# Three score tiles of 1024 keys, and one PSUM bank each for projection and value sums, in a hybrid attention block

## The chip, the cores and the metric

The kernel runs on one core of one Trainium2 chip. The metric is the device time of the program in microseconds (us). The engines are named as in the profile: PE is TensorE's matrix products, PEld its weight loads, DVE is VectorE, ACT ScalarE, POOL GpSimd, SP SyncE (which here only issues DMAs). PE writes its sums into PSUM, which has eight banks of 512 floats for each of its 128 partitions; DVE and ACT read them from there ("drain" them), after which a bank may be filled anew.

## The reference, cut to what matters

One layer over 2048 positions of width 1024, all in float32:

```python
u = rms_norm(x, norm1_w)
dq, dk, dv, sq, sk, sv = split(u @ w_in)
# four heads: two softmax maps each, chunk-causal mask, relative-position bias
attn = softmax(q0 @ k0 * s + bias) - lam * softmax(q1 @ k1 * s + bias)
y_A = rms_norm(attn @ dv) * (1 - lambda_init)
# eight heads of stick-breaking attention, strictly causal
log_1mb = log_sigmoid(-z)                       # z = q @ k * scale
rem = cumsum(log_1mb, reverse=True) - log_1mb
y_B = rms_norm(exp(log_sigmoid(z) + rem) @ sv)
h = x + concat(y_A, y_B) @ w_out
u2 = rms_norm(h, norm2_w)
out = h + (silu(u2 @ w_gate) * (u2 @ w_up)) @ w_down
```

## The kernel before, in words

Matrix products run on 16-bit operands. A float32 operand is split into a high and a low half, and a product of two such operands is three products (high-high, high-low, low-high) summed in one PSUM bank.

**Groups and blocks.** The 2048 queries are 16 blocks of 128 (`i`). The heads are eight groups (`g`): groups 0 to 3 are one differential head each, groups 4 to 7 a pair of stick-breaking heads each. For each group the normalized, transposed input is projected in 16 tiles of 128 positions: `proj_tile` (L314) lets PE make 24 products of 128x384 into a bank with the tag `pj` (L320), and `proj_out` (L334) drains it: the values first (L327 or L329 for the high half, L330 for the low half), then the queries and keys (L341 or L343 in groups 0 to 3, again L327/L329 and L330 in groups 4 to 7). Which of ACT and DVE makes a high half is chosen by a balance of estimated load. In group 0 the input itself is transposed on the way (`fresh_t`, L607; `transposed`, L591, with L594 on PE).

**Scores.** `score_chunk` (L446) multiplies the queries of a block with up to 512 keys (two products, L448) into a bank with the tag `sc`, of which there are four. A block sees the keys up to its own end, taken in stretches of 1024 keys (`b`), and a stretch in chunks of 512 (`c`). The chunks are what the change is about.

- Differential attention (`probs`, L462): DVE copies each chunk out of PSUM with the running maximum (L483; L487 for the last 256 keys, which get the bias); then an exponential on ACT, the difference of the two maps on DVE, and `split_t` (L398), which makes the two halves (L89, L91 or L93 and L98) and transposes them by a DMA into `aT`.
- Stick-breaking attention (`stage_a`, L540): for each chunk ACT makes two sigmoids (L554 into SBUF, L555 in place in PSUM), DVE runs the product from the right as a scan (L557), then multiplies (L558), chunk by chunk from the right. The chunks hang together by one column (`om[:, hi : hi + 1]`). Then `split_t`.

**Value sums.** `pv` (L453) multiplies `aT` with the values into a bank with the tag `yp`, of which there are two (L458); four query blocks share a bank (two in the last group), at 128 columns each. After the fourth block `finish` (L407) takes the squares of the bank (L416 or L418), scales it into `y` (L429), transposes `y` back into the same bank (L431), and drains that to 16 bits (`mo`, L435 on ACT, L436 on DVE).

**PSUM before.** Two banks `pj` (also used by the small sums that set the weights' scales and by the output projection's `po`, L755), four banks `sc` (also used by `transposed`), two banks `yp` (also used once by `build_bias`). In the feed-forward part the six banks of `sc` and `yp` are a ring with the tag `b`, and every fourth call of `pst` (L816) takes a bank `pj`.

**The order of the work.** The program is written as generators. `advance` (L708) emits projection tiles of later groups between the attention blocks, about eight tiles ahead. Then a scheduler that simulates the engines sets the order of the instructions on each engine from these, with priorities (`PRI`), from its own idea of durations and of when each buffer comes free: so the number of banks changes the order. On the chip each engine runs its list strictly in order and waits for semaphores.

The stages follow each other with some overlap. By the trace of the profile the prologue (projection of group 0) lies in 0 to 105 us, differential attention in 105 to 615 us, the stick-breaking attention of groups 4 to 6 (with the beginning of 7) in 615 to 1215 us, the last group with the output projection (`out_proj`, L744, products L761) in 1215 to 1472 us, and the feed-forward part to the end.

Of the kernel before, what the change touches and what calls it, by code (L numbers as in the profile page):

```python
# [11 lines left out]
F32 = mybir.dt.float32  # L12
# [4 lines left out]
ALU = mybir.AluOpType  # L17
# [42 lines left out]
def block(tc, a, out):  # L60
# [3 lines left out]
    with top:  # L64
# [182 lines left out]
        psj = top.enter_context(tc.tile_pool(name="psj", bufs=2, space=PSUM, side="right"))  # L247
# [3 lines left out]
        with ExitStack() as ph1:  # L251
# [4 lines left out]
            bias = s16p.tile([P, 4, 256], F32, name="bias", bufs=1)  # L256

# [202 lines left out]
            def diff_attn(g, G):  # L460
                @pri("at")
                def probs(i):  # L462
# [8 lines left out]
                    for m in range(2):  # L471
                        nx = 0
                        for b in range(nb):
                            n = min(1024, L - 1024 * b)
                            z = z4()
                            for c in range((n + 511) // 512):
                                lo, hi = 512 * c, min(512 * c + 512, n)
                                sc = ps.tile([P, 512], F32, tag="sc", bufs=4, name=nm("sc"))
                                score_chunk(G, sc, i, 2 * b + c, m, (hi - lo) // P)
                                f = min(max(near - 1024 * b - lo, 0), hi - lo)  # L480
                                note("D", 1.05 * (hi - lo) + 200)
                                if f > 0:
                                    DVE.tensor_scalar(z[:, lo : lo + f], sc[:, :f], kz_d[:], None, op0=ALU.mult, op1=ALU.max, accum_out=mx[:, m, nx : nx + 1])  # L483
                                    nx += 1
                                if f < hi - lo:
                                    b0 = 1024 * b + lo + f - (i - 1) * 128
                                    DVE.tensor_tensor_reduce(z[:, lo + f : hi], sc[:, f : hi - lo], bias[:, g, b0 : b0 + hi - lo - f], kz_d[:], -3.0e38, ALU.add, ALU.max, mx[:, m, nx : nx + 1])  # L487
                                    nx += 1
                            zs[m].append((b, n, z))
# [46 lines left out]
            def sb_attn(g, G):  # L536
                last = {}

                @pri("at")
                def stage_a(i, m, b):  # L540
                    L = (i + 1) * 128
                    n = min(1024, L - 1024 * b)
                    be, om = z4(), z4()
                    if b == i // 8:
                        DVE.memset(om[:, n : n + 1], 8192.0)
                    else:
                        DVE.tensor_copy(om[:, n : n + 1], last[m][:, 0:1])
                    last[m] = om
                    for c in range((n - 1) // 512, -1, -1):
                        lo, hi = 512 * c, min(512 * c + 512, n)  # L550
                        w = hi - lo
                        sc = ps.tile([P, 512], F32, tag="sc", bufs=4, name=nm("sc"))
                        score_chunk(G, sc, i, 2 * b + c, m, w // P, b == i // 8 and hi == n)
                        ACT.activation(om[:, lo:hi], sc[:, :w], AF.Sigmoid, scale=G["nkz"][:])  # L554
                        ACT.activation(sc[:, :w], sc[:, :w], AF.Sigmoid, scale=G["kz"][:])  # L555
                        ov = om[:, lo:hi][:, ::-1]
                        DVE.tensor_tensor_scan(ov, ov, sc[:, :w], om[:, hi : hi + 1], op0=ALU.mult, op1=ALU.bypass)  # L557
                        DVE.tensor_tensor(be[:, lo:hi], sc[:, :w], om[:, lo + 1 : hi + 1], ALU.mult)  # L558
                        note("A", 1.7 * w + 400)
                        note("D", 3.15 * w + 350)  # L560
                    return n, split_t(be[:, :n], n, "A", "P")
# [3 lines left out]
                def stage_b(i, m, b, n, aT):  # L565
                    r, k = fq(g, i)
                    if i // k not in ypd:
                        ypd[i // k] = ps.tile([P, 512], F32, tag="yp", name=nm("yp"))
# [22 lines left out]
            def transposed(xn, o):  # L591
                tr = ps.tile([P, 512], F32, tag="sc", bufs=4, name=nm("xtr"))
                for j in range(4):
                    PE.transpose(tr[:, P * j : P * j + P], xn[:, o + P * j : o + P * j + P], id32[:])  # L594
                return tr
# [29 lines left out]
            def build_bias():  # L625
# [5 lines left out]
                for h in range(4):  # L631
                    pt = ps.tile([P, 512], F32, tag="yp", name=nm("bt"))
# [111 lines left out]
            def out_proj():  # L744
                for t in range(NT):
# [8 lines left out]
                    for h in range(2):  # L754
                        po = psj.tile([P, 512], F32, tag="pj", name=nm("po"))  # L755
# [47 lines left out]
        with ExitStack() as ph2:  # L803
# [424 lines left out]
```

## Time and profile before

| | us |
|---|---|
| runs of the kernel | 2783.66, 2777.36, 2782.47 |
| median | 2782.47 |
| span of the profiled execution | 2785.0 |
| busy in it: PE, DVE, POOL, ACT | 2489.9, 2000.8, 1445.2, 1361.8 |
| of it PE on projection products (L320, 3072 of them) | 572.3 |
| of it DVE on the scan (L557, 320 of them) | 355.5 |

The profile is of one execution, and its span of 2785.0 us is that execution's own time, from the first instruction to the last; all times in the trace count from its start. A row of the timeline has the start of an instruction (or of a run of equal ones), how long it took, the engine and line, what it wrote and read with the shapes, and in brackets how long the engine had stood idle before it and whose result it waited for. A row by form has the busy time in all, the mean in ns of one, and the idle time before them. A row of the windows has the stretch, its length, the busy time and count of instructions of PE, PEld, DVE, ACT and POOL in this order, the granted clock of PE as a share of full speed, the share of time that the DMA engines were busy, and GB/s. A row of waits has who waited for whom: the idle time in all, how often, and the longest.

### The profile page before, as it was taken

What the parts mean: (1) busy time and instruction counts of PE and PEld (TensorE: products, weight loads), DVE (VectorE), ACT (ScalarE), POOL (GpSimd) and SP (SyncE); (2) the same over time, 40 slices, a digit from 0 to 9 for tenths busy, and PEclk for the clock granted to TensorE, in tenths of its full rate; (3) what the DMA queues carried; (4) which work ended last, traced back from release to release, by engine and by line L of the source; (5) the groups of instructions that cost most, each with busy time, mean ns of one, the idle gap of its engine ahead of it and who ended that gap; (6) DMA issues with size and microseconds to landing.
All of it is one profiled execution on the core that took longest, in us unless ns stands there. A gap on an engine that the chain in (4) does not pass through costs nothing. (4 is left out here: it accounts for less than half of the span.)

```text
span 2785.0 us, 45469 instructions
## 1 busy us (share of the span) xinstructions
PE 2489.9 (89%) x17084; PEld 1409.0 (51%) x17084; DVE 2000.8 (72%) x3782; ACT 1361.8 (49%) x2543; POOL 1445.2 (52%) x1008
## 2 busy tenths in 40 slices
PE   6998989888878786888889798989999999999998
PEld 4665556555545453557775343444444444444443
DVE  6888879687989989876756877777786644434445
ACT  4665656466878788765644534443442212111121
POOL 2567767665544555546665656565654332322323
PEclk9999999999999897999999999999999999999999
DMA  6788787789999998997796565655658844635534
GB/s 225 199 167 184 147 188 163 164 174 205 198 205 198 192 182 160 190 198 205 197 309 253 184 235 189 221 187 191 240 170 299 327 155 178 227 125 190 211 129 166
DMA packets 649133, 551.91 MB, mean 198 GB/s; under 512 B 506624, under 2 KB 574208, under 8 KB 638672
## 3 DMA queue, kind: packets, MB, share of 16 engines
q1 hardware_dynamic: 647088, 546.92, 71.2%
q8 instruction: 134, 2.20, 0.3%
q0 software_dynamic: 512, 1.36, 0.2%
q10 hardware_dynamic: 1312, 0.72, 0.1%
q14 instruction: 87, 0.71, 0.1%
HBM read 265.27 MB, written 151.52 MB: 150 GB/s over the span
## 5 line engine op out<-in xcount | busy, mean ns | idle before, releaser
L98 POOL TENSOR_TENSOR s<-z,s 128x1024 f16<-128x1024 f32 (+7 forms) x288 | 474.1, 1654 | 334.8 <-ACT s L89 299.3
L320 PE MATMUL pj<-w,xt 128*128 128x384 f16 x3072 | 572.3, 334 | 32.6 <-DVE st L330 11.6
L320 PEld LDWEIGHTS <-xt 128*128 128x128 f16 x3072 | 299.9, 100 | 241.8 <-issue 36.3
L448 PE MATMUL sc<-kT,qT 128*128 128x512 f16 (+3 forms) x1280 | 346.9, 362 | 74.6 <-DVE z L558 34.4
L1034 PE MATMUL pd<-wd,act 128*128 128x512 f16 x1848 | 406.2, 379 | 3.3 <-DVE hs L1040 2.4
L557 DVE TENSOR_TENSOR_SCAN z<-z,sc 128x512 f32<-128x512 f32 (+3 forms) x320 | 355.5, 1112 | 68.6 <-ACT sc L555 65.1
L458 PE MATMUL yp<-v,aT 128*128 128x64 f16 (+1 forms) x4896 | 281.2, 207 | 80.0 <-DMA aT<-s 79.2
L458 PEld LDWEIGHTS <-aT 128*128 128x128 f16 x4896 | 245.2, 102 | 169.4 <-DMA aT<-s 105.1
L936 PEld LDWEIGHTS <-wg 128*128 128x128 f16 x1848 | 183.9, 100 | 264.3 <-issue 58.8
L98 POOL TENSOR_TENSOR hs<-hs,cu 128x512 f32<-128x512 f32 x132 | 170.5, 1297 | 238.2 <-DVE cu L1040 82.6
L936 PEld LDWEIGHTS <-wu 128*128 128x128 f16 x1848 | 181.0, 98 | 222.1 <-issue 9.0
L1034 PEld LDWEIGHTS <-act 128*128 128x128 f16 x1848 | 180.6, 98 | 222.6 <-issue 4.7
L98 POOL TENSOR_TENSOR act<-cg,act 128x512 f16<-128x512 f32 x117 | 160.8, 1385 | 247.7 <-ACT act L992 141.5
L98 POOL TENSOR_TENSOR fst<-fst 128x512 f32<-128x512 f32 x97 | 179.6, 1852 | 167.6 <-DVE wd L215 78.6
L1040 DVE SCALAR_TENSOR_TENSOR hs<-pd,c,hs 128x512 f32<-128x512 f32 x192 | 142.1, 748 | 160.8 <-PE pd L1034 159.1
L89 ACT CAST s<-z 128x384 f16<-128x384 f32 (+7 forms) x216 | 170.1, 788 | 151.5 <-DMA aT<-s 56.4
L554 ACT ACTIVATE z<-sc,c 128x512 f32<-128x512 f32 (+3 forms) x320 | 202.6, 633 | 10.6 <-PE sc L448 6.5
L558 DVE TENSOR_TENSOR z<-sc,z 128x512 f32<-128x512 f32 (+3 forms) x320 | 193.3, 606 | 8.1
L992 ACT CAST act<-cg 128x512 f16<-128x512 f32 x132 | 80.6, 617 | 234.2 <-DVE cg L998 190.9
L555 ACT ACTIVATE sc<-sc,c 128x512 f32<-128x512 f32 (+3 forms) x320 | 194.8, 609 | 0.0
L761 PE MATMUL po<-wo,mt 128*128 128x256 f16 x1536 | 181.3, 276 | 11.0 <-DVE xf L764 6.3
L936 PE MATMUL pm<-X,wg 128*128 128x512 f16 x792 | 179.1, 379 | 1.2 <-ACT bx L1109 1.2
(233 smaller groups left out, 4028.4 us busy)
## 6 DMA issues: line engine op xcount, KB each, us to landing
xt<-xs SPq DMA_DIRECT2D x112, 512.0 KB, 4.4
hs<-hd SPq DMA_DIRECT2D x96, 512.0 KB, 4.3
hd<-hs SPq DMA_DIRECT2D x80, 512.0 KB, 3.2
split<-wg SPq DMA_DIRECT2D x11, 1792.0 KB, 10.5
split<-wu SPq DMA_DIRECT2D x11, 1792.0 KB, 10.3
split<-wd SPq DMA_DIRECT2D x11, 1792.0 KB, 10.4
wg<-split SPq DMA_DIRECT2D x11, 1792.0 KB, 7.3
wd<-split SPq DMA_DIRECT2D x11, 1792.0 KB, 8.4
```

The costliest lines, as they stand in the source:

```text
L89: ACT.copy(dst, src)
L98: (DVE if e == "D" else POOL).tensor_tensor(dst, a_, b_, op)
L320: PE.matmul(pj[:, :384], lhsT=xv[:, xi, kt, :], rhs=G["w"][:, wi, kt, :], start=n == 0, stop=n == 23)
L448: PE.matmul(sc[:, : 128 * w].rearrange("p (t n) -> p t n", n=P), lhsT=G["q"][i // 4][:, 2 - 2 * o + m, i % 4, :], rhs=G["k"][q][:, m, 0:w, ...
L458: PE.matmul(yp[:, y0 : y0 + wd], lhsT=aT[:, a_, :], rhs=v[:, v_ : v_ + wd], start=start and j == 0 and q == 0, stop=stop and j == nb - 1 a ...
L554: ACT.activation(om[:, lo:hi], sc[:, :w], AF.Sigmoid, scale=G["nkz"][:])
L555: ACT.activation(sc[:, :w], sc[:, :w], AF.Sigmoid, scale=G["kz"][:])
L557: DVE.tensor_tensor_scan(ov, ov, sc[:, :w], om[:, hi : hi + 1], op0=ALU.mult, op1=ALU.bypass)
L558: DVE.tensor_tensor(be[:, lo:hi], sc[:, :w], om[:, lo + 1 : hi + 1], ALU.mult)
L761: PE.matmul(po[:, sl], lhsT=mt[:, kt, P * xi : P * xi + P], rhs=wos[2 * h + n][wi][:, kt, :], start=q == 0, stop=q == 23)
L936: PE.matmul(ps_[:].rearrange("p (t n) -> p t n", n=P), lhsT=wv[:, wo, wi, 128 * kt : 128 * kt + 128], rhs=X[xo][:, :, xi, kt, :], start=st ...
L1034: PE.matmul(po[:], lhsT=act[:, ao, xi, 128 * j : 128 * j + 128], rhs=W["d"][:, wo, wi, :], start=start and u == 0 and q == 0, stop=u == nu ...
```

## The change

The banks are dealt out anew: one bank `pj` instead of two, one bank `yp` instead of two, and three score tiles of 1024 floats (two banks each) in place of four of 512. A score tile now holds a whole stretch of up to 1024 keys. PE's products stay at up to 512 columns each, so their number is the same; what DVE and ACT do to the scores (L483, L487, L554, L555, L557, L558) is issued once for each tile and no longer for each chunk. `transposed` takes a score tile and uses half of it. Of the output projection's two half sums one takes the bank `pj` and the other a score tile for the first twelve blocks; the last four take theirs from `pst`. The feed-forward part has a ring of seven, and every eighth call of `pst` takes the bank `pj`. Behind the first added lines the numbers of the lines are shifted by 1 to 6.

```diff
-        psj = top.enter_context(tc.tile_pool(name="psj", bufs=2, space=PSUM, side="right"))
+        psj = top.enter_context(tc.tile_pool(name="psj", bufs=1, space=PSUM, side="right"))
...
+            def scores():
+                return ps.tile([P, 1024], F32, tag="sc", bufs=3, name=nm("sc"))
...
-                            z = z4()
+                            z, sc = z4(), scores()
                             for c in range((n + 511) // 512):
                                 lo, hi = 512 * c, min(512 * c + 512, n)
-                                sc = ps.tile([P, 512], F32, tag="sc", bufs=4, name=nm("sc"))
-                                score_chunk(G, sc, i, 2 * b + c, m, (hi - lo) // P)
-                                f = min(max(near - 1024 * b - lo, 0), hi - lo)
-                                note("D", 1.05 * (hi - lo) + 200)
-                                if f > 0:
-                                    DVE.tensor_scalar(z[:, lo : lo + f], sc[:, :f], kz_d[:], None, op0=ALU.mult, op1=ALU.max, accum_out=mx[:, m, nx : nx + 1])
...
+                                score_chunk(G, sc[:, lo:hi], i, 2 * b + c, m, (hi - lo) // P)
+                            f = min(max(near - 1024 * b, 0), n)
+                            note("D", 1.05 * n + 200)
+                            if f > 0:
+                                DVE.tensor_scalar(z[:, :f], sc[:, :f], kz_d[:], None, op0=ALU.mult, op1=ALU.max, accum_out=mx[:, m, nx : nx + 1])
...
-                        ypd[0] = ps.tile([P, 512], F32, tag="yp", name=nm("yp"))
+                        ypd[0] = ps.tile([P, 512], F32, tag="yp", bufs=1, name=nm("yp"))
...
+                    sc = scores()
                     for c in range((n - 1) // 512, -1, -1):
                         lo, hi = 512 * c, min(512 * c + 512, n)
-                        w = hi - lo
-                        sc = ps.tile([P, 512], F32, tag="sc", bufs=4, name=nm("sc"))
-                        score_chunk(G, sc, i, 2 * b + c, m, w // P, b == i // 8 and hi == n)
-                        ACT.activation(om[:, lo:hi], sc[:, :w], AF.Sigmoid, scale=G["nkz"][:])
-                        ACT.activation(sc[:, :w], sc[:, :w], AF.Sigmoid, scale=G["kz"][:])
-                        ov = om[:, lo:hi][:, ::-1]
-                        DVE.tensor_tensor_scan(ov, ov, sc[:, :w], om[:, hi : hi + 1], op0=ALU.mult, op1=ALU.bypass)
-                        DVE.tensor_tensor(be[:, lo:hi], sc[:, :w], om[:, lo + 1 : hi + 1], ALU.mult)
...
+                        score_chunk(G, sc[:, lo:hi], i, 2 * b + c, m, (hi - lo) // P, b == i // 8 and hi == n)
+                    ACT.activation(om[:, :n], sc[:, :n], AF.Sigmoid, scale=G["nkz"][:])
+                    ACT.activation(sc[:, :n], sc[:, :n], AF.Sigmoid, scale=G["kz"][:])
+                    ov = om[:, :n][:, ::-1]
+                    DVE.tensor_tensor_scan(ov, ov, sc[:, :n], om[:, n : n + 1], op0=ALU.mult, op1=ALU.bypass)
+                    DVE.tensor_tensor(be[:, :n], sc[:, :n], om[:, 1 : n + 1], ALU.mult)
...
             def transposed(xn, o):
-                tr = ps.tile([P, 512], F32, tag="sc", bufs=4, name=nm("xtr"))
+                tr = scores()
...
-                        po = psj.tile([P, 512], F32, tag="pj", name=nm("po"))
+                        if t < 12 and h:
+                            po = scores()[:, :512]
+                        elif t < 12:
+                            po = psj.tile([P, 512], F32, tag="pj", name=nm("po"))
+                        else:
+                            po = pst("po")
...
-                if pst_n[0] % 4:
-                    return ps2.tile([P, 512], F32, tag="b", bufs=6, name=nm(t))
+                if pst_n[0] % 8:
+                    return ps2.tile([P, 512], F32, tag="b", bufs=7, name=nm(t))
```

Since the scheduler reads the buffers, the order of the instructions changes nearly everywhere in the attention. Three places show how.

The first is on PE, where one projection tile (`pj`) ends and the next begins. In the kernel before, in group 0 at the start of differential attention, the last product of one tile stands directly ahead of the first of the next:

```order
L448 LDWEIGHTS qT_739
L448 MATMUL sc_1470<-kT_740,qT_739 128x256
L320 LDWEIGHTS xt_1141
L320 MATMUL pj_1185<-w_172,xt_1141 128x384
L320 LDWEIGHTS xt_1422
L320 MATMUL pj_1427<-w_817,xt_1422 128x384
```

In the changed kernel, in the prologue, three runs of transposes (which are on score tiles) stand between two tiles:

```order
L323 LDWEIGHTS xt_409
L323 MATMUL pj_478<-w_172,xt_409 128x384
L595 MATMUL sc_590<-id_63,z_581 128x128 x4
L595 MATMUL sc_597<-id_63,z_581 128x128 x4
L595 MATMUL sc_643<-id_63,z_634 128x128 x4
L323 LDWEIGHTS xt_462
L323 MATMUL pj_552<-w_172,xt_462 128x384
```

With one bank the scheduler puts other work between a tile and the next where it has some.

The second place is on PE as well, where the value bank is handed over after the first four blocks of group 0. In the kernel before, the value products of the next four blocks (`yp_1488`, the second bank) stand ahead of the transposes of `y` of the first four (`yp_1280`):

```order
L458 LDWEIGHTS aT_1486
L458 MATMUL yp_1488<-v_284,aT_1486 128x128
L431 MATMUL yp_1280<-id_63,y_1401 128x128 x4
L448 LDWEIGHTS qT_1005
L448 MATMUL sc_1760<-kT_507,qT_1005 128x512
```

In the changed kernel the last score and projection products stand there instead, and the next value product comes 65 rows behind these:

```order
L451 MATMUL sc_1740<-kT_740,qT_1005 128x512
L323 LDWEIGHTS xt_1418
L323 MATMUL pj_1423<-w_817,xt_1418 128x384
L434 MATMUL yp_1280<-id_63,y_1397 128x128 x4
L451 LDWEIGHTS qT_1005
L451 MATMUL sc_1747<-kT_1006,qT_1005 128x256
```

The value products that stood ahead of the transposes have moved behind them, and behind the drain of `yp_1280`.

The third place is on DVE in group 4, query block 12 (the scan is listed there as SCALAR_TENSOR_TENSOR of L557, L558 in the changed kernel). Before, scans and multiplies of 512 and 128 columns, with the drains of a projection tile (`pj_10254`) between them:

```order
L545 MEMSET z_9525 128x1
L557 SCALAR_TENSOR_TENSOR z_9478<-z_9478,sc_9488 128x512
L330 SCALAR_TENSOR_TENSOR v_10014<-pj_10254,v_10014 128x2x64
L558 TENSOR_TENSOR z_9477<-sc_9488,z_9478 128x512
L557 SCALAR_TENSOR_TENSOR z_9525<-z_9525,sc_9527 128x128
L330 SCALAR_TENSOR_TENSOR st_10013<-pj_10254,st_10013 128x4x64
L558 TENSOR_TENSOR z_9524<-sc_9527,z_9525 128x128
L547 COPY z_9591<-z_9478 128x1
L557 SCALAR_TENSOR_TENSOR z_9525<-z_9525,sc_9535 128x512
L558 TENSOR_TENSOR z_9524<-sc_9535,z_9525 128x512
```

In the changed kernel:

```order
L547 MEMSET z_9158 128x1
L558 SCALAR_TENSOR_TENSOR z_9158<-z_9158,sc_9160 128x640
L559 TENSOR_TENSOR z_9157<-sc_9160,z_9158 128x640
L547 MEMSET z_9200 128x1
L558 SCALAR_TENSOR_TENSOR z_9200<-z_9200,sc_9202 128x640
L333 SCALAR_TENSOR_TENSOR v_9127<-pj_9231,v_9127 128x2x64
L559 TENSOR_TENSOR z_9199<-sc_9202,z_9200 128x640
L549 COPY z_9261<-z_9158 128x1
L333 SCALAR_TENSOR_TENSOR st_9126<-pj_9231,st_9126 128x4x64
L558 SCALAR_TENSOR_TENSOR z_9261<-z_9261,sc_9263 128x1024
L559 TENSOR_TENSOR z_9260<-sc_9263,z_9261 128x1024
```

The 512 and 128 of a stretch of 640 keys have become one instruction, and the next stretch is one of 1024; the drains of a projection tile (`pj_9231`) still stand between single scans and multiplies.

More of the change, by code (lines that the diff above doesn't have):

```diff
@@ L567, in stage_b @@
                     if i // k not in ypd:
-                        ypd[i // k] = ps.tile([P, 512], F32, tag="yp", name=nm("yp"))
+                        ypd[i // k] = ps.tile([P, 512], F32, tag="yp", bufs=1, name=nm("yp"))
                     yp = ypd[i // k]
@@ L591, in transposed @@
             def transposed(xn, o):
-                tr = ps.tile([P, 512], F32, tag="sc", bufs=4, name=nm("xtr"))
+                tr = scores()
                 for j in range(4):
                     PE.transpose(tr[:, P * j : P * j + P], xn[:, o + P * j : o + P * j + P], id32[:])
-                return tr
+                return tr[:, :512]
             @pri("fr")
@@ L631, in build_bias @@
                 for h in range(4):
-                    pt = ps.tile([P, 512], F32, tag="yp", name=nm("bt"))
+                    pt = ps.tile([P, 512], F32, tag="yp", bufs=1, name=nm("bt"))
                     PE.matmul(pt[:, :384], lhsT=rbb[:, h, :], rhs=oh[0:32, 0:384], start=True, stop=True)
```

14 lines of the change are left out of this document (7 added, 7 removed).

## Prediction

> **What bounds the kernel now.** I read the windows first, cut at the borders of the stages, then two stretches inside the stick-breaking stage:
>
> ```profile
> 0.00:105.00 105.00, 76.89 (x449) 49.70 (x450) 73.14 (x162) 50.73 (x102) 39.24 (x48) 0.93 0.67 215
> 105.00:615.00 510.00, 463.64 (x3628) 295.79 (x3626) 431.98 (x1302) 305.18 (x795) 353.95 (x253) 0.97 0.80 171
> 615.00:1215.00 600.00, 475.90 (x4891) 299.71 (x4888) 528.96 (x952) 467.68 (x905) 306.34 (x199) 0.93 0.96 194
> 1215.00:1472.00 257.00, 229.84 (x2364) 194.50 (x2365) 172.31 (x279) 138.78 (x221) 153.69 (x101) 0.97 0.84 233
> 1472.00:2785.00 1313.00, 1243.60 (x5759) 569.33 (x5756) 794.45 (x1090) 399.41 (x522) 592.01 (x407) 0.98 0.56 203
> ...
> 932.00:982.00 50.00, 33.16 (x384) 20.79 (x383) 47.34 (x73) 40.90 (x71) 28.16 (x15) 0.83 0.94 172
> 1038.00:1112.00 74.00, 46.37 (x483) 26.84 (x484) 70.57 (x107) 63.23 (x110) 40.94 (x25) 0.77 0.87 160
> ```
>
> The feed-forward part is PE's (1244 of 1313 us), the stage ahead of it too (230 of 257). Differential attention is led by PE (464 of 510, 91%), with DVE at 85%. Stick-breaking attention is led by DVE (529 of 600, 88%), PE stands at 79%. In the last two stretches DVE is at 95%, PE at 66 and 63%: there DVE alone sets the pace, and DVE is known to reach 95% where nothing else holds it up. Then the waits, first of differential attention, then of stick-breaking attention:
>
> ```profile
> PEld L458 <- DMA aT<-s: 36.2, 24, 4.2
> ...
> DVE z L483 <- PE sc L448: 18.7, 20, 3.1
> ```
>
> ```profile
> PEld L458 <- DMA aT<-s: 56.3, 50, 3.8
> ...
> PEld L448 <- DVE z L558: 44.3, 40, 2.1
> ...
> DVE z L557 <- ACT sc L555: 35.9, 42, 3.2
> ```
>
> PE waits for transposed probabilities, and in the second stage 44.3 us for a score bank that DVE still holds; DVE waits for sigmoids there.
>
> **Part 1: fewer DVE instructions.** The forms give a fixed cost:
>
> ```profile
> L557 DVE TENSOR_TENSOR_SCAN z<-z,sc 128x512 f32<-128x512 f32 x224 | 284.9, 1272 | 40.4 <-ACT sc L555 38.0 <-PE pj L320 1.6 <-PE sc L450 0.4
> L558 DVE TENSOR_TENSOR z<-sc,z 128x512 f32<-128x512 f32 x224 | 153.4, 686 | 5.6
> ...
> L557 DVE TENSOR_TENSOR_SCAN z<-z,sc 128x128 f32<-128x128 f32 x32 | 15.2, 473 | 15.7 <-ACT sc L555 15.4
> L558 DVE TENSOR_TENSOR z<-sc,z 128x128 f32<-128x128 f32 x32 | 9.2, 288 | 0.8
> ```
>
> ```profile
> L557 DVE TENSOR_TENSOR_SCAN z<-z,sc 128x512 f32<-128x512 f32 x183 | 232.8, 1272 | 20.6 <-ACT sc L555 18.1 <-PE pj L320 1.6 <-PE sc L450 0.4
> ```
>
> ```profile
> L483 DVE TENSOR_SCALAR_CACHE_REDUCE z<-sc,c 128x512 f32<-128x512 f32 x168 | 122.6, 742 | 14.4 <-PE sc L448 12.7 <-POOL s L93 1.0 <-POOL s L98 0.5
> L483 DVE TENSOR_SCALAR_CACHE_REDUCE z<-sc,c 128x128 f32<-128x128 f32 x32 | 10.9, 341 | 1.4 <-POOL s L98 1.4
> ```
>
> The scan goes from 473 to 1272 ns over 384 columns, 2.08 ns a column, so 207 ns at none; the multiply in the same way 155 ns. Two chunks merged save one of each: 0.362 us. Scans fall from 320 to 192, so there are 128 merges; 183 of the 224 scans of 512 columns lie in 615 to 1215 us, which puts 128 x 183/224 = 105 merges there: 38 us, DVE 529 to 491. L483 has 207 ns at no column; 96 of 256 go: 20 us, but in differential attention, where PE leads, so off the path (price zero; 10 if half of it counted). ACT's two sigmoids also lose 128 issues each; ACT stands at 468 of 600, behind DVE, so this is no term of its own.
>
> The Trainium skill ("Perfetto Trace Analysis", section "Optimizing Scalar/DVE Operations") gives the fixed part as some 60 ns on SBUF and 125 on PSUM and says that grouping helps a saturated engine, while an engine that isn't saturated may do better with smaller pieces; an estimate by its figures is 105 x 0.185 = 19 us in place of 38. Rows here say twice that.
>
> What is the 38 us worth? At the present DVE share of 88% the stage takes 491/0.88 = 557 us, 43 less. It could take more of the gain, if the share rises (rival 1).
>
> **Part 2: one bank for projections.** A tile's 24 products take 4.06 us; until its drains end no product of the next tile can start now. PE runs its list in order, so scores, values and SP's and POOL's later steps behind that product wait with it. From the timelines of PE and ACT, prologue and differential attention:
>
> ```profile
> 63.14 3.58 PE L320 MATMUL pj<-w,xt 128*128 128x384 f16 x21
> 66.55 1.04 PE L594 MATMUL xtr<-id,z 128*128 128x128 f32 x8
> 67.42 4.06 PE L320 MATMUL pj<-w,xt 128*128 128x384 f16 x24
> ```
>
> ```profile
> 97.12 0.28 ACT L327 ACTIVATE v<-pj 128x128 f16<-128x128 f32 x1 [2.73 <-PE pj L320]
> ...
> 99.41 0.38 ACT L341 ACTIVATE raw<-pj 128x256 f32<-128x256 f32 x1 [1.05 <-DVE v L330]
> ```
>
> ```profile
> 401.86 0.28 ACT L327 ACTIVATE v<-pj 128x128 f16<-128x128 f32 x1 [0.92 <-PE pj L320]
> 403.70 0.38 ACT L341 ACTIVATE raw<-pj 128x256 f32<-128x256 f32 x1 [1.57 <-DVE v L330]
> ...
> 404.55 0.33 PE L320 MATMUL pj<-w,xt 128*128 128x384 f16 x1
> ...
> 409.67 0.36 ACT L341 ACTIVATE raw<-pj 128x256 f32<-128x256 f32 x1
> ```
>
> The drain takes, from the last product, 99.79 - 97.12 = 2.7 us in the prologue, and in differential attention 404.08 - 401.86 = 2.2 or 410.03 - 404.88 = 5.1. What covers it is work placed between two tiles. Before, 51 of 127 boundaries had none. In the changed order I counted the products between and priced them by their durations here: on average 1.3 us in the prologue (eight transposes are 67.42 - 66.55 = 0.87), 2.6 in differential attention, 2.9 in the stick-breaking stage.
>
> - Prologue: 13 boundaries x (2.7 - 1.3) = +18. No bank is spare there, and PE leads (the bounds: 0 if another wait covers it, 13 x 2.7 = 35 if no cover is in time).
> - Differential attention: 51 boundaries, each between 0 (drain 2.2, cover 2.6) and 5.1 - 2.6 = 2.5; I take 0.8, nearer to the short drain since a scheduler that knows of the one bank has put the drains early: +41 (0 to 128).
> - Stick-breaking attention: here a drain takes longer,
>
> ```profile
> 840.31 0.81 PE L320 MATMUL pj<-w,xt 128*128 128x384 f16 x4
> ...
> 849.61 0.41 DVE L330 SCALAR_TENSOR_TENSOR st<-pj,st 128x256 f16<-128x256 f32 x1
> ...
> 982.60 3.41 PE L320 MATMUL pj<-w,xt 128*128 128x384 f16 x20 [1.27 <-DVE st L330]
> ```
>
> 850.02 - 841.12 = 8.9 us, since DVE puts scans first; even with two banks PE waited for one at 982.60. But what waits is PE, and DVE leads. DVE has enough in hand: a merged tile is 2 x 1272 - 207 + 2 x 686 - 155 = 3.55 us of it, two tiles wait in the ring of three while one is filled: 7.1 us, against 4.06 of projection products and what is left of the drain. And the new order puts the drains between single scans, where the old one had long runs of scans without one (the two 95% stretches above). So 0 here (up to +288, rival 2).
>
> **Part 3: one bank for value sums.** From the last value product to the end of the last drain of the bank:
>
> ```profile
> 459.29 0.55 PE L458 MATMUL yp<-v,aT 128*128 128x128 f16 x7
> ...
> 470.53 0.67 DVE L429 TENSOR_TENSOR y<-yp,yrs 128x512 f32<-128x512 f32 x1
> ...
> 475.92 0.74 DVE L436 SCALAR_TENSOR_TENSOR mo<-yp,c,mo 128x512 f16<-128x512 f32 x1
> ```
>
> 476.66 - 459.84 = 16.8 us. Before, 29 of 35 next value products began inside that time in the other bank; now none can. Up to 471.20 the transposes wait as they did. New is the rest, 5.5 us at most, once in four blocks; the new order has 0.2 to 18 us of PE work there. Differential attention has 16 such places: between 0 and 16 x 5.3 = 85, I take 0.6 each, +10. In the other stage DVE's lead covers it as above. From both terms of differential attention (51) I take off 11: of the 36.2 us that PE waits for `aT` there, a third is time in which `aT` would land during the new waits. So +40 (0 to 190).
>
> **Part 4: the rest.** The score ring's three tiles hold 3072 columns for 2048: part of the 44.3 us of waits for a score bank goes, but DVE leads there, so nothing beyond part 1. SP's and POOL's steps are the same ones in the same number. In the stage from 1215 on the output projection's two half sums have a bank each as before,
>
> ```profile
> L761 PE MATMUL po<-wo,mt 128*128 128x256 f16 x1536 | 181.3, 276 | 11.0 <-DVE xf L764 6.3
> ```
>
> and PE waits 6.3 us for their drain now; +2 for the score tiles being shared with the last group (0 to 10). In the feed-forward part each call of `pst` reuses the bank of eight calls before, with 6 + 2 as with 7 + 1: 0.
>
> **The sum.** +18 + 40 - 43 + 2 + 0 = +17: a span of 2785 + 17 = 2802 us. The median of the runs shown is 2782.5, 2.5 below that span; so **2799 us**. Its own bounds: the prologue's 0 to 35 and the other terms of its size give 2788 to 2835. About 0.2% (5.6 us) is what a measurement of this kernel can tell from no change.
>
> **Rivals.**
>
> 1. *Faster: DVE alone sets the stick-breaking stage.* The evenly mixed order and the deeper ring let DVE run at the 95% of the two stretches: 491/0.95 = 517, -83; with prologue and differential attention at half their price, +30, this is 2785 - 83 + 30 = 2732 of span; with both at full price 2762; with the 2.5 off, some 2750 us between. For it: those stretches. Against it: DVE waits 35.9 us for sigmoids, and these now cover 1024 keys before a scan can begin. Chance 0.37 (with what lies between it and no change).
> 2. *Much slower: one projection bank stops PE in the stick-breaking stage.* If a drain stays at 8.9 us with 2.9 covered, each of the 48 boundaries stops PE for 6 us, and scores and values queue behind it: 288, so PE needs 476 + 288 = 764 us for a stage of 600. With half of the boundaries so it is 476 + 144 = 620, +20, and with prologue, differential stage and the 2 beside it 2785 + 20 + 60 = 2865; with all 3009. I put it at 2880. It decides from the point where PE's stops exceed 557 - 476 = 81 us, 1.7 a boundary. For it: PE's granted clock in the 66 and 63% stretches is 0.83 and 0.77, so that a PE that often stops is also a slower one. Against: the order that mixes drains with scans. The Trainium skill ("Perfetto Trace Analysis", section "Matmuls") says that independent groups of products should rotate through PSUM banks, so that the drain of one overlaps the products of the next, which is this case. Chance 0.11.
> 3. *No change within 0.2%*, the prologue's and the differential stage's price and the saving cancelling: 2777 to 2788. Chance 0.10.
>
> **How the numbers follow.** The forecast has 0.42, rival 1 0.37, rival 2 0.11, rival 3 0.10. Faster is 0.37, same 0.10, slower 0.42 + 0.11 = 0.53. The range takes in the forecast's own (2788 to 2835), rival 3, the greater part of rival 1 down to 2740, and goes up to 2865 for dearer drains; it leaves out the deepest gains and most of rival 2.
>
> **What would show it.** In the profile after: the prologue some 18 us longer, with waits of PE (L323) for the drains L333 and L344 that aren't there now; the differential stage some 40 longer by the same waits; DVE's busy time in the stick-breaking stage down by 38, its share still near 88%, the stage shorter by some 40; the feed-forward part as long as before. The forecast is wrong if the prologue and the differential stage keep their lengths (drains hidden), or if DVE's share rises to 95% (rival 1), or if the stick-breaking stage gets longer with PE waiting for L333 (rival 2).

## The result, and the profile after

The changed kernel takes 3005.7 us (median; 3002.2 to 3009.7), the kernel before 2783.1 in the same comparison: 1.0809 times as long, 95% interval 1.0793 to 1.0825, or 223 us more. The forecast was 2799, the range 2740 to 2865.

For the comparison both executions are cut anew at the same events: the first score product of groups 0, 4 and 7, and the last product of the output projection. Windows of before, then of after:

```profile
0.00:106.00 106.00, 77.89 (x456) 50.30 (x457) 74.10 (x162) 50.73 (x103) 39.24 (x48) 0.94 0.68 216
106.00:614.00 508.00, 462.13 (x3612) 294.67 (x3610) 430.01 (x1295) 304.17 (x793) 353.95 (x253) 0.97 0.80 171
614.00:1134.00 520.00, 412.39 (x4281) 260.49 (x4282) 466.73 (x827) 413.32 (x786) 269.15 (x170) 0.93 0.96 191
1134.00:1472.00 338.00, 293.85 (x2982) 234.24 (x2981) 235.54 (x410) 194.13 (x342) 190.88 (x130) 0.96 0.86 228
```

```profile
0.00:125.00 125.00, 86.11 (x455) 53.03 (x456) 73.64 (x162) 51.76 (x103) 40.55 (x49) 0.92 0.63 198
125.00:696.00 571.00, 474.28 (x3568) 295.07 (x3567) 421.44 (x1067) 304.17 (x791) 352.45 (x252) 0.94 0.67 147
696.00:1292.00 596.00, 440.60 (x4288) 271.84 (x4286) 450.89 (x633) 382.57 (x590) 269.59 (x171) 0.88 0.82 166
1292.00:1697.00 405.00, 317.85 (x3025) 246.90 (x3025) 242.90 (x363) 194.61 (x289) 180.79 (x127) 0.91 0.73 196
1697.00:3003.60 1306.60, 1244.64 (x5759) 569.12 (x5756) 789.06 (x1082) 395.55 (x520) 591.82 (x407) 0.98 0.56 203
```

The prologue is longer by 19 us, differential attention by 63, stick-breaking attention of groups 4 to 6 by 76, the last group with the output projection by 67; the feed-forward part is 6 shorter. In the third row no engine leads any more: PE is busy 441 of 596 us, DVE 451 (76%, 90% before). PE's granted clock is lower in the first four rows (0.88 for 0.93 in the third), and for the same instructions PE is busy 2563.5 us in all, 74 more.

By form, the merged scan and multiply:

```profile
L558 DVE TENSOR_TENSOR_SCAN z<-z,sc 128x1024 f32<-128x1024 f32 x80 | 187.6, 2344 | 66.6 <-ACT sc L556 62.6
L559 DVE TENSOR_TENSOR z<-sc,z 128x1024 f32<-128x1024 f32 x80 | 97.4, 1218 | 1.5
```

Two scans of 512 took 2 x 1272 = 2544 ns, so one merge saves 200; two multiplies 1372, so it saves 154: 0.354 us for the 0.362 of the forecast. But DVE's busy time falls by less. In groups 4 to 6, where 96 of the 128 merges lie, it goes from 466.7 to 450.9 us, 0.16 us a merge, because the durations of neighbours overlap, as here in the changed kernel:

```profile
1154.01 2.35 DVE L558 TENSOR_TENSOR_SCAN z<-z,sc 128x1024 f32<-128x1024 f32 x1 [0.43 <-ACT sc L556]
...
1156.27 0.40 DVE L333 SCALAR_TENSOR_TENSOR st<-pj,st 128x256 f16<-128x256 f32 x1
```

The scan ends at 1156.36, 0.09 us after the drain behind it has begun. An instruction that is saved gives back its duration less this overlap. The Trainium skill ("Perfetto Trace Analysis", section "Optimizing Scalar/DVE Operations") says of its 60 and 125 ns that they are engine-busy times and that the latency in the profile is about twice as long. This trace agrees: the prediction's estimate by these figures, 0.185 us a merge, is near the 0.16 of busy time, and twice that is near the 0.354 of the forms.

The waits of the whole execution, before and after:

```profile
DVE z L557 <- ACT sc L555: 65.1, 55, 7.2
ACT v L327 <- PE pj L320: 56.3, 35, 5.8
...
DVE v L330 <- ACT v L327: 21.1, 14, 4.1
PE pj L320 <- DVE st L330: 11.6, 11, 1.7
...
PE pj L320 <- ACT raw L341: 1.7, 1, 1.7
```

```profile
ACT v L330 <- PE pj L323: 181.8, 58, 8.4
DVE z L558 <- ACT sc L556: 117.1, 63, 7.7
DVE v L333 <- ACT v L330: 96.1, 33, 10.3
...
PE pj L323 <- DVE st L333: 48.4, 27, 5.0
PE pj L323 <- ACT raw L344: 38.9, 21, 5.8
```

PE waits for the drains of a projection tile 87 us (13 before). That was expected in kind. What was not: ACT waits 182 us for a projection tile to drain (56 before), and DVE 96 us for ACT's first drain (21). These waits aren't spread over the stages as the lost time is. Of the 182 us, 34 are in the prologue, 93 in differential attention, 48 in groups 4 to 6 and 7 behind them; of the 96 us, 19, 44, 31 and 2. In groups 4 to 6 alone the rows are, before and after:

```profile
DVE z L557 <- ACT sc L555: 30.1, 37, 3.2
DVE v L330 <- ACT v L327: 4.7, 3, 3.4
...
ACT v L327 <- PE pj L320: 4.3, 7, 1.2
...
PE pj L320 <- DVE st L330: 7.4, 8, 1.4
```

```profile
DVE z L558 <- ACT sc L556: 73.4, 45, 5.1
DVE v L333 <- ACT v L330: 30.9, 11, 6.8
...
ACT v L330 <- PE pj L323: 48.3, 19, 6.4
...
PE pj L323 <- DVE st L333: 37.3, 20, 5.0
```

DVE, which led this stage before, now waits there most of all for sigmoids and next for ACT at the drains. A stretch of the timeline of after, in the stick-breaking attention of group 6, shows PE, ACT and DVE standing for each other in turn:

```profile
1160.34 1.22 DVE L559 TENSOR_TENSOR z<-sc,z 128x1024 f32<-128x1024 f32 x1
1160.74 0.65 PE L323 MATMUL pj<-w,xt 128*128 128x384 f16 x3
...
1162.59 0.27 ACT L330 ACTIVATE v<-pj 128x128 f16<-128x128 f32 x1
1162.89 0.29 DVE L333 SCALAR_TENSOR_TENSOR v<-pj,v 128x128 f16<-128x128 f32 x1 [1.32 <-ACT v L330]
1163.22 0.38 ACT L330 ACTIVATE st<-pj 128x256 f16<-128x256 f32 x1 [0.36 <-DVE v L333]
1163.63 0.42 DVE L333 SCALAR_TENSOR_TENSOR st<-pj,st 128x256 f16<-128x256 f32 x1 [0.45 <-ACT st L330]
1164.20 5.74 PE L323 MATMUL pj<-w,xt 128*128 128x384 f16 x24 [2.20 <-DVE st L333]
...
1169.98 0.28 ACT L330 ACTIVATE v<-pj 128x128 f16<-128x128 f32 x1 [6.38 <-PE pj L323]
1170.29 0.29 DVE L333 SCALAR_TENSOR_TENSOR v<-pj,v 128x128 f16<-128x128 f32 x1 [6.23 <-ACT v L330]
...
1171.60 0.65 PE L323 MATMUL pj<-w,xt 128*128 128x384 f16 x3 [0.26 <-DVE st L333]
```

PE stops 2.20 us for four drains that go back and forth between ACT and DVE, then makes the next tile; ACT and DVE have that tile's drains next in their lists and stand 6.38 and 6.23 us. No scores are in hand for DVE then: the scan and multiply of the last filled score tile are done at 1161.56, and PE makes no score product from 1152.2 to 1175.3. The window of just this tile:

```profile
1164.00:1170.00 6.00, 5.80 (x32) 3.19 (x33) 0.06 (x1) 0.02 (x1) 0.88 (x1) 0.72 1.13 209
```

DVE works 0.06 of 6 us, ACT 0.02, and the clock granted to PE is 0.72: the 24 products take 5.74 us, where they took 4.06 in the prologue before.

### The profile page after: what moved, and what is told of

The parts are those of the page before. It is cut to its first block, busy times and chain, and to the rows that moved or that the text cites. A ratio compares the mean times of both kernels' runs of the same rounds, so it can differ in the third digit from the quotient of the medians.

```text
span 3003.6 us, 44676 instructions
## 1 busy us (share of the span) xinstructions
PE 2563.5 (85%) x17084; PEld 1436.0 (48%) x17084; DVE 1977.9 (66%) x3305; ACT 1328.7 (44%) x2288; POOL 1435.2 (48%) x1004
## 3 DMA queue, kind: packets, MB, share of 16 engines
q10 hardware_dynamic: 1312, 0.72, 0.1%
## 5 line engine op out<-in xcount | busy, mean ns | idle before, releaser
L323 PE MATMUL pj<-w,xt 128*128 128x384 f16 x3072 | 599.0, 352 | 92.2 <-DVE st L333 48.4
L323 PEld LDWEIGHTS <-xt 128*128 128x128 f16 x3072 | 316.2, 105 | 343.5 <-issue 153.8
L558 DVE TENSOR_TENSOR_SCAN z<-z,sc 128x128 f32<-128x128 f32 (+7 forms) x192 | 330.7, 1722 | 128.8 <-ACT sc L556 117.1
L451 PE MATMUL sc<-kT,qT 128*128 128x512 f16 (+3 forms) x1280 | 322.2, 372 | 104.2 <-DVE z L547 51.4
L461 PE MATMUL yp<-v,aT 128*128 128x64 f16 (+1 forms) x4896 | 247.6, 210 | 91.3 <-DMA aT<-s 72.5
L461 PEld LDWEIGHTS <-aT 128*128 128x128 f16 x4896 | 227.6, 103 | 135.9 <-DMA aT<-s 89.3
L451 PEld LDWEIGHTS <-qT 128*128 128x128 f16 x1280 | 116.1, 102 | 207.2 <-DVE z L547 50.9
L555 ACT ACTIVATE z<-sc,c 128x128 f32<-128x128 f32 (+7 forms) x192 | 166.5, 867 | 32.5 <-PE sc L451 24.4
L559 DVE TENSOR_TENSOR z<-sc,z 128x128 f32<-128x128 f32 (+7 forms) x192 | 174.4, 909 | 6.4
L942 PE MATMUL pm<-X,wu 128*128 128x512 f16 x792 | 178.5, 379 | 0.0
```

The lines of the kernel that those rows point to most:

```text
L323: PE.matmul(pj[:, :384], lhsT=xv[:, xi, kt, :], rhs=G["w"][:, wi, kt, :], start=n == 0, stop=n == 23)
L451: PE.matmul(sc[:, : 128 * w].rearrange("p (t n) -> p t n", n=P), lhsT=G["q"][i // 4][:, 2 - 2 * o + m, i % 4, :], rhs=G["k"][q][:, m, 0:w, ...
L461: PE.matmul(yp[:, y0 : y0 + wd], lhsT=aT[:, a_, :], rhs=v[:, v_ : v_ + wd], start=start and j == 0 and q == 0, stop=stop and j == nb - 1 a ...
L555: ACT.activation(om[:, :n], sc[:, :n], AF.Sigmoid, scale=G["nkz"][:])
L558: DVE.tensor_tensor_scan(ov, ov, sc[:, :n], om[:, n : n + 1], op0=ALU.mult, op1=ALU.bypass)
L559: DVE.tensor_tensor(be[:, :n], sc[:, :n], om[:, 1 : n + 1], ALU.mult)
```

## The experiments

The first question was which part costs what. Theory P: the single projection bank. Rivals: V, the single value bank; W, the whole tile of 1024 keys, for whose sigmoids a scan must wait. All medians are of runs compared with the kernel before on the same chip (2780.0 to 2784.0 there).

For the runs that carry the argument, these are the lengths of the stages in us, from their traces, cut at the same events as above:

| | prologue | groups 0 to 3 | groups 4 to 6 | group 7, output projection | feed-forward |
|---|---|---|---|---|---|
| kernel before | 106 | 508 | 520 | 338 | 1313 |
| changed kernel | 125 | 571 | 596 | 405 | 1307 |
| one projection bank alone | 129 | 556 | 612 | 415 | 1308 |
| one value bank alone | 112 | 503 | 544 | 348 | 1312 |
| changed banks without the merging | 116 | 589 | 624 | 399 | 1307 |
| merging alone | 115 | 509 | 579 | 366 | 1315 |
| order of one projection bank, with two | 115 | 540 | 560 | 430 | 1305 |
| the same with the wait | 122 | 584 | 593 | 425 | 1305 |

**One projection bank alone.** The output projection's second half sum in a score bank, the last four blocks' in `pst`, and the ring of seven come with it.

```diff
-        psj = top.enter_context(tc.tile_pool(name="psj", bufs=2, space=PSUM, side="right"))
+        psj = top.enter_context(tc.tile_pool(name="psj", bufs=1, space=PSUM, side="right"))
```

> The kernel before (2783 us) with one projection bank alone; scores by chunks of 512 in four banks and two value banks as before (the feed-forward ring of seven and the output projection's second half sum in a score bank come with it). Theory P (the single projection bank couples PE with DVE and ACT and is most of the 222 us): 2930 us or more, with waits of PE for the drains of L330 and L341 of over 80 us. Rival W (the whole tile of 1024 is the price: a scan waits for sigmoids over 1024 keys): at most 2830. Rival V (the single value bank): at most 2830.

3033.2 us, 1.0886 times before (1.0862 to 1.0911): +249, more than the whole change. Its waits:

```profile
ACT v L327 <- PE pj L320: 153.6, 53, 8.3
...
DVE v L330 <- ACT v L327: 101.5, 34, 8.4
...
PE pj L320 <- ACT raw L341: 30.2, 21, 6.9
PE pj L320 <- DVE st L330: 25.1, 26, 2.1
```

P holds in time. But PE's own waits for the drains are 55 us, not over 80; ACT's and DVE's at the drain are the larger rows. In groups 4 to 6 this run is 92 us longer than the kernel before, though no score is merged in it, and DVE waits 70 us for sigmoids there (30 before). What comes with the bank acts behind group 6, so the bank is enough to take DVE's lead away.

**One value bank alone.**

```diff
-                        ypd[0] = ps.tile([P, 512], F32, tag="yp", name=nm("yp"))
+                        ypd[0] = ps.tile([P, 512], F32, tag="yp", bufs=1, name=nm("yp"))
```

> The kernel before (2783 us) with one value bank alone. Theory P: 2775 to 2805. Rival W: the same. Rival V: 2900 or more, with PE's value products waiting for the drain of the bank (mo, L436) for over 50 us.

2822.7 us, 1.0136 (1.0117 to 1.0156): +39. Above P's 2805 and far below V's 2900: a price of its own, but the small one. PE's value products wait 6.3 us for the drain of the bank (L436), where V expected over 50. By the table nothing of the price lies in differential attention and 24 us lie in groups 4 to 6.

**The changed banks without the merging.** One bank for projections, one for values, six score banks of 512, each chunk by itself.

```diff
-                                sc = ps.tile([P, 512], F32, tag="sc", bufs=4, name=nm("sc"))
+                                sc = ps.tile([P, 512], F32, tag="sc", bufs=6, name=nm("sc"))
```

> The banks of the changed kernel (one for projections, one for values), but six score banks of 512 and every chunk worked off by itself as before: the changed kernel (3006 us) without the merging. Theory P: 2970 to 3050, above the changed kernel by what merging saves or about as long as it. Rival W: 2850 or less. Rival V: like P.

3038.5 us, 1.0917 (1.0900 to 1.0934). The changed kernel is 33 us below it: that is what merging brings among these banks, most of it (28 us) in groups 4 to 6, with DVE's busy time 2020.1 here and 1977.9 there. W falls, as far as it says that whole tiles are the price.

**The merging alone.** The changed kernel's code with the banks of before, so two score tiles of 1024.

```diff
-                return ps.tile([P, 1024], F32, tag="sc", bufs=3, name=nm("sc"))
+                return ps.tile([P, 1024], F32, tag="sc", bufs=2, name=nm("sc"))
```

> The merging alone: two score tiles of 1024 in the place of four banks of 512, two projection banks and two value banks as before. Theory P: 2740 to 2800 (38 us of DVE saved in the stick-breaking stage, against a ring of two tiles only). Rival W: 2900 or more, with DVE's waits for sigmoids over 100 us.

2880.7 us, 1.0333 (1.0312 to 1.0355): +97. DVE's waits for sigmoids:

```profile
DVE z L558 <- ACT sc L556: 133.6, 78, 7.6
```

P expected 2740 to 2800 and is wrong here; W's sign is over 100 us, though its 2900 isn't reached. With two tiles merging is a loss, and in eight banks the third tile leaves one bank each for projections and values. Whether the 97 us are the short ring or the longer chain by itself, this run doesn't separate.

The second question was how one bank costs 249 us when PE waits only 55 for it. Theory Q: it is PE's wait after all. Theory O: it is the order; the lists of ACT and DVE hold a tile's drains where these engines must stand for it.

**The order of one bank, with two banks.** The kernel before, with an edge for the scheduler from the drains of a tile to the first product of the next, which makes no wait on the chip. The output projection's half sums are placed as in the changed kernel in this run too.

```diff
+                        while drains:
+                            tc.add_manual_dep(mm.ins, drains.pop(0).ins.name, mybir.DependencyInfo(mybir.DependencyClass.NoSync, mybir.DependencyReason.DATA), reason="one at a time")
```

> The banks of the kernel before (two for projections), but the scheduler is told that the first product of a projection tile comes after all drains of the tile before; on the chip nothing waits for that, only the order of the lists is that of one bank. Theory O (it is the order: the drains stand early in the lists of ACT and DVE, and these stand still there for PE's projection tile): 2930 us or more, with ACT's waits at L327 for PE over 120 us. Theory Q (it is PE's own wait for the bank): 2830 or less.

2950.2 us, 1.0601 (1.0582 to 1.0619): +167, though no wait of PE for a drain of a projection tile shows in its trace. The waits at the drain in this kernel:

```profile
ACT v L331 <- PE pj L322: 123.4, 38, 10.4
DVE v L334 <- ACT v L331: 73.9, 24, 11.1
```

**The same with the wait.** The same edge as one that PE waits for on the chip (`Sync` for `NoSync`).

> As the order-only kernel, but PE also waits on the chip for the drains, as with one bank. Both theories: 3000 to 3060 us, as the kernel with one projection bank alone (3033). The difference to the order-only kernel is the wait by itself: under O less than 70 us, under Q 150 or more.

3029.8 us, 1.0882 (1.0860 to 1.0905), as the real single bank (3033). Of its price 167 of 247 us stand without the wait and 80 more come with it. O expected less than 70 for the wait, Q 150: O is near, and PE's wait is a real second part. But not all of the 167 us is the order of tile and drains. By the table the order alone costs 81 us up to the end of group 6, and with the wait it is 165, so there order and wait have half each. The other large part, 92 us (87 with the wait), lies behind group 6, where ACT's waits for projection tiles hardly grow. There the output projection is placed in other banks in this run, in the run of one projection bank (77 longer there), in the changed banks without the merging (61) and in the changed kernel (67); the two runs above that leave it as it was are 10 and 28 longer. That placing alone was not tried, so how much of the last attention stage is its doing is open.

**Drains early, among the changed banks.**

```diff
-PRI = {"sc": 0, "spl": 0, "pv": 0, "fin": 0, "pm": -200, "po": 0, "pb": 0, "lw": 0, "fr": 0, "at": 200, "ox": 0, "wm": 0}
+PRI = {"sc": 0, "spl": 0, "pv": 0, "fin": 0, "pm": -200, "po": 400, "pb": 0, "lw": 0, "fr": 0, "at": 200, "ox": 0, "wm": 0}
```

> The changed kernel (3006 us) with the drains of a projection tile scheduled at a high priority, so that they stand as early as they can. Theory O: no faster than 2990, since ACT and DVE stand there as long or longer. Theory Q: 2930 or less, since the bank comes free earlier.

3002.0 us, 1.0772 (1.0745 to 1.0799): no gain to speak of, in O's range. But ACT's waits at L330 fall to 156 us (182 without the priority), where O expected them as long or longer, and PE's for the drains only to 81 (87). The bank hardly came free earlier, so the run says little against Q.

**One copy for the drain, among the changed banks.**

```diff
+                px = sp.tile([P, 384], F32, tag="px", bufs=1, name=nm("px"))
+                ACT.copy(px[:], pj[:, :384])
+                note("A", 480)
+                pj = px
```

> The changed kernel (3006 us) with one copy of the whole projection tile by ACT into SBUF (some 0.5 us, 128 of them), from which the halves are then made: PE's bank comes free after one instruction. Theory Q: 2880 or less. Theory O: 2930 to 3020, since ACT still stands in line at the copy; DVE's wait for ACT's high half moves off the bank.

2931.1 us, 1.0525 (1.0508 to 1.0543): 75 us back, just inside O's range. The waits:

```profile
ACT px L340 <- PE pj L323: 98.1, 34, 7.0
...
PE pj L323 <- ACT px L340: 45.7, 36, 4.0
DVE v L333 <- ACT v L330: 18.9, 15, 2.5
```

DVE no longer stands at the drain (18.9 us, 96.1 before the copy); ACT still does, and PE waits for it.

**Drains early or late, in the kernel before.** Is it that drains stand early (O), or that tile and drains must take strict turns (O')? The kernel before with only `"po"` in that table set to 400, then to -400.

> The kernel before (2783 us), all its banks kept, with only the drains of a projection tile scheduled at a high priority. Theory O as far as it says that drains early in the lists are the price: 2810 us or more, with ACT's waits for PE at L327 over 90 us (56 before). Theory O', that the price is the strict turn of tile and drains, one after the other, however early: 2770 to 2800.

> The kernel before with only the drains at a low priority. Theory O: 2740 to 2785, since ACT and DVE stand less at the drains. Theory O': 2770 to 2810.

2780.7 us, 0.9998 (0.9986 to 1.0010), and 2785.7 us, 1.0019 (1.0009 to 1.0029). The second is just above O's 2785. With two banks it hardly matters where the scheduler would like the drains. ACT's waits with the early drains are 43.2 us, fewer than before:

```profile
ACT v L327 <- PE pj L320: 43.2, 26, 6.8
```

O in its first form falls. O' fits: together with the two runs with the edge, this speaks for the strict turn, tile, drains, tile, in three lists that are each worked off in order.

**The order of one value bank, with two.** The same kind of edge from the drains of `mo` to the next value products.

```diff
+                        while mos:
+                            tc.add_manual_dep(mm.ins, mos.pop(0).ins.name, mybir.DependencyInfo(mybir.DependencyClass.NoSync, mybir.DependencyReason.DATA), reason="one at a time")
```

> The banks of the kernel before (two for values), but the scheduler is told that the first value product of the next blocks comes after the drain of the value bank before; on the chip nothing waits for it. The kernel with one value bank is 39 us slower than before. If for values too it is the order of the lists: 2805 to 2830 us. If it is the wait for the bank: 2775 to 2800.

2801.0 us, 1.0063 (1.0043 to 1.0083): +20 of the value bank's 39, just between the two expectations. Here too order and wait have about half each.

**Sigmoids by chunks, among the changed banks.** Scan and multiply stay merged.

```diff
-                    ACT.activation(om[:, :n], sc[:, :n], AF.Sigmoid, scale=G["nkz"][:])
-                    ACT.activation(sc[:, :n], sc[:, :n], AF.Sigmoid, scale=G["kz"][:])
+                        ACT.activation(om[:, lo:hi], sc[:, lo:hi], AF.Sigmoid, scale=G["nkz"][:])
+                        ACT.activation(sc[:, lo:hi], sc[:, lo:hi], AF.Sigmoid, scale=G["kz"][:])
```

> The changed kernel (3006 us) with the two sigmoids by chunks of 512 again, so that ACT begins when the first half of a tile is there; the scan and the multiply stay merged. If DVE's waits for the sigmoids of a whole tile (117 us) are a price of their own: 2985 or less, with those waits under 95 us. If they follow from the turn of tile and drains: 2995 to 3030.

3246.1 us, 1.1665 (1.1646 to 1.1684): outside both expectations, 240 us over the changed kernel. The order shows what it did: the scheduler pulled the two halves of a tile's filling apart. In PE's list of this kernel, group 4, one tile's first half is followed by its second only 68 rows later, with half of the next tile (`sc1683`) between, where the changed kernel has the four products of most tiles together:

```
10767 L451 MATMUL sc1676_9884<-kT1565_9015,qT1564_9014 128x512
10769 L451 MATMUL sc1676_9884<-kT1565_9015,qT1564_9014 128x512
...
10777 L451 MATMUL sc1683_9956<-kT1371_7807,qT1564_9014 128x512
...
10837 L451 MATMUL sc1676_9884<-kT1488_8458,qT1564_9014 128x512
```

So half-filled tiles hold the ring of three. DVE waits 315.8 us for sigmoids in this run, where the expectation was under 95 if they had a price of their own. In the window of that place DVE is busy 7.2 of 16 us, and the clock is 0.50:

```profile
960.00:976.00 16.00, 6.78 (x56) 3.87 (x57) 7.20 (x7) 7.48 (x11) 4.25 (x2) 0.50 0.44 94
```

The run says nothing, then, on what whole-tile sigmoids cost by themselves. No version that was tried beats the kernel before.

## Why the prediction was wrong, point by point

1. **DVE's saving per merge: right by form, half as large in busy time.** A merge saves 0.354 us of durations for the forecast's 0.362, but 0.16 us of DVE's busy time: 16 us in groups 4 to 6, where 96 merges at 0.362 would give 35. The term of -43 was too large for this reason alone, and DVE's share didn't hold at 88% but fell from 90 to 76% there. Among the changed banks merging is worth 33 us of the whole.
2. **The prologue: the number right, the cause in part**, +19 for +18. PE waits 9.5 us for the drain L344 there (none before) and doesn't wait for L333. The rest is other waits and slower products; with two projection banks the merging alone has the prologue at 115 us, 9 longer, too. So the match is partly luck.
3. **Differential attention: the mechanism there, the size short**, +63 for +40. The forecast's own terms come to some 27 of the 63: PE waits 31 us for the drains of projection tiles (4 before), 5 for the value bank, and 5 less for `aT`. PE's busy time grows by another 12 at a lower clock (0.94 for 0.97), and the rest is other waits, for score banks and for `qT` among them. The bounds given, 0 to 190, don't follow from their parts, which add up to 0 to 202 after the 11 taken off.
4. **Stick-breaking attention: the step that failed.** "But what waits is PE, and DVE leads. DVE has enough in hand", and so 0 for the projection bank there. The bank alone makes groups 4 to 6 longer by 92 us (612 for 520); in the changed kernel they are 76 longer, where a gain was forecast. DVE did not have enough in hand: in the changed kernel it waits 73 us there for sigmoids (30 before) and 31 for ACT at the first drain (5 before), and it is idle for 145 of 596 us (53 of 520 before). The step counted the ring's two tiles as full whenever PE stops. In the window of 6 us above no score tile was filled at all, and the drain stood next in DVE's list, so it worked 0.06. The forecast counted the new order of the drains as a relief; in the order-only run an order of strict turns costs 40 us in groups 4 to 6, and with the wait on the chip it is 73.
5. **The stage behind group 6: +67 for +2.** The forecast put only the score tiles' sharing here. ACT's waits for projection tiles don't grow in this stage (7 us for 6). The largest wait of PE that is new is for the input of the transposes (L595, waiting for DVE's L223): 26 us, where it was 4. What brings it is open, as said with the order-only run.
6. **The value bank: +39 alone** for +10 in differential attention and nothing else. Alone it costs nothing in differential attention (503 us for 508) and 24 us in groups 4 to 6, where it was taken as covered by DVE's lead, the same failed step.
7. **The feed-forward part: right**, -6 for 0.

Rival 2 had the place and the sign (0.11), and its price with all 48 boundaries, 3009 us, is close to 3006, but not by its sum: it let PE stop 288 us in the stick-breaking stage, and counted on more than 81 before the stage grows. PE waits 37 us for these drains in groups 4 to 6 (87 in the whole run), and the stage grew all the same, with DVE and ACT standing too. The Trainium skill's rule cited with it ("Perfetto Trace Analysis", section "Matmuls"), that independent groups of products should rotate through PSUM banks, agrees with the run of one projection bank: 249 us more, 163 of them up to the end of group 6.

Rival 1 needed DVE at 95%; it fell to 76%.

What stays open: how the 97 us of the merging alone divide into the short ring and the longer chain; what the output projection's new placing costs in the stage behind group 6; and how much of the order's 167 us is the lower clock (mean granted 0.945 there, 0.966 before). PE is busy 2552.8 us in that run, 63 more than before.

## What to carry to other kernels

An accumulation tile with one bank puts its producer and everyone who drains it into strict turns; where each engine works off a fixed list, the drain is a place at which the leading engine too must stand, so its work in hand behind that place is no cover. To price a lost second buffer, ask for every engine in the turn (tile plus drain) how long it will stand, and not only for the producer: here PE's own waits for the drains were 55 us of a price of 249. Price merged small instructions by the busy time that they save, which here was half of what the durations by form say, and price the buffer that is taken for it first: 33 us against 249 and 39.

## What was not expected of the hardware

PE's granted clock is lower where PE stops more: in groups 4 to 6 it was 0.93 with PE busy 79% of the time before and 0.88 with 74% after, in the feed-forward part 0.98 with 95%. It fell to 0.72 in the 6 us of the window above, behind a stop of 2.20 us, and to 0.50 in the last experiment's window. In the first of these 24 products took 5.74 us, and 4.06/0.72 = 5.64, so a slowed product lengthens the turn further. Over the whole run PE's 74 us more on the same instructions match its mean granted clock (0.966 before, 0.939 after): 2489.9 x 0.966 = 2405 and 2563.5 x 0.939 = 2407. That the stops bring the clock down is argued from these rows, not shown by a run of its own.
